# A two-layer DeltaNet backbone on one core: scaling on GpSimd, other store queues, and a TensorE order fixed only from a layer's second latent phase on

## The chip, the cores and the metric

The kernel runs on one core of a Trainium2 chip. The metric is the device time of one execution in microseconds, as a median over runs.

## The reference

Two layers. Each normalises 2048 latent and 256 context tokens (1024 features), projects them once, and feeds a short gated convolution and a bidirectional gated DeltaNet with 4 heads of 128; both results go through one output projection and are added to the tokens. Cut to what matters here:

```python
def hybrid_layer(xl, xc, c, c_ctx, ..., col_major, ctx_out):
    hl = rms_norm(xl, norm_w) * (1.0 + scale_l) + shift_l      # xl (1, 2048, 1024)
    hc = rms_norm(xc, norm_w) * (1.0 + scale_c) + shift_c      # xc (1, 256, 1024)
    pl = split_proj(to_scan_order(hl, col_major) @ w_in)
    pc = split_proj(hc @ w_in)
    dl = deltanet_inputs(pl[4], pl[5], pl[6], pl[8], pl[9], conv_qkv, a_log, dt_bias, seg_l)
    dc = deltanet_inputs(pc[4], pc[5], pc[6], pc[8], pc[9], conv_qkv, a_log, dt_bias, seg_c)
    ol, oc = bidirectional_gdn(dl, dc, ctx_out)     # latent scans start from the context's final state
    yl = from_scan_order(branch_outputs(pl, ol, conv_a, gdn_norm, seg_l), col_major)
    xl = xl + gate_l * (yl @ w_out)
    ...

def deltanet_inputs(q, k, v, ...):
    qkv = jax.nn.silu(segment_conv(jnp.concatenate([q, k, v], axis=-1), conv_qkv, seg))
    q, k, v = jnp.split(qkv, ...)
    q = l2_normalize(q.reshape(b, n, N_HEADS_DN, HEAD_DK)) * (HEAD_DK ** -0.5)
    k = l2_normalize(k.reshape(b, n, N_HEADS_DN, HEAD_DK))
    ...
```

The factor `nk` of the change is the reciprocal norm of `l2_normalize(k)`.

## The kernel before

Feature tiles lie on 128 partitions. The tokens form five chunks: 0 is the context (256 tokens), 1 and 2 are the first half of the latent tokens (512 each), 3 and 4 the second. A layer runs two calls of `phase` (the first with the context and chunks 1 and 2, the second with chunks 3 and 4: the second latent phase) and then `output`. In a phase, a unit is 128 columns of `w_in`: `split` loads them (L313, into `raw`, two buffers), ScalarE rounds them to `whi` (L314), GpSimd and VectorE form the rest `wlo` (L316), and `project` does 24 matmuls for each chunk (`h` by `whi`, `l` by `whi`, `h` by `wlo`, `d<-...` in the rows) into one of three PSUM banks `d`. A consumer then empties the bank; for q, k and v it is a convolution (L339 to L343), a SiLU (L540, L541) and a store to DRAM (`rec_d<-y`, L542). `prep` turns normalised tokens (`xx`) into the operands `h` and `l`: transposes on TensorE (`c<-ident,xx`), L427 on ScalarE (`hf`), and a rounding and a subtraction (L433).

Between the projections' steps run jobs. The job J{l}c has 8 items, J{l}0 to J{l}3 have 16 each; an item is 128 tokens of one head, and there are 144 in the kernel. In `delta` an item loads q, k, v from `rec_d` (L636, L637, ring of four `rec` tiles, two items ahead) and decay rows (L639), transposes them into a PSUM bank `t` (there are two `t` banks), forms key products, and copies the transposes back into `rec`: L668 sums the squares of k, L669 and L670 (a pow on GpSimd) make the norm's factor `nk` from them, L674 copies, L675 copies with the factor `nk`, L677 puts a product in. L678 stores `rec` on ScalarE's queue. Then small triangular systems are solved (`Lt`, `X`; L735, L737), whose tiles of 1024 columns have the tag `m4` (two buffers). The jobs F{l}a to F{l}c and C{l} are scans over the chunks' states. `out_weights` loads `w_out` in two halves of four row tiles into `raw` (L966), rounds them (L967) and forms the rest (L968).

TensorE's order is written by hand over the whole kernel, in one `tc.manual_schedule` over this engine (L1163): it executes in the order in which the code emits, which `phase` and the jobs' `yield`s set by a running count of TensorE's own time (`Order.now`). The order on the other engines and on SP's queue comes from the Tile scheduler, and is fixed once the kernel is built.

Of the kernel before, what the change touches and what calls it, by code (L numbers as in the profile page):

```python
# [8 lines left out]
F32 = mybir.dt.float32  # L9
# [3 lines left out]
ALU = mybir.AluOpType  # L13
# [50 lines left out]
def hybrid_backbone_kernel(ctx_stack: ExitStack, tc: tile.TileContext,  # L64
# [346 lines left out]
    def prep(L, p, i, xx, keep):  # L411

        P = L.P
        r = 1 if p == 0 else 0
        hi, lo = L.hs[p]
        o = slice(128 * i, 128 * i + 256)
        for k2 in range(0, KT, 2):
            with urgent():
                ps = pscan(("c0", "c1")[k2 // 2 % 2]) if p else pt()
                for dk in range(2):  # L420
                    for j in range(2):
                        c_ = 256 * dk + 128 * j
                        turn(ps[:, c_:c_ + 128], xx[:, j, 128 * (k2 + dk):128 * (k2 + dk) + 128])
                hf = side([128, 2, 256], "hf")
                for dk in range(2):
                    k = k2 + dk
                    nc.scalar.activation(hf[:, dk, :], ps[:, 256 * dk:256 * dk + 256], AF.Identity,  # L427
                                         scale=P["am"][:, k, r:r + 1], bias=P["mod"][:, k, r:r + 1])
                if keep:
                    nc.sync.dma_start(out=L.h_d[:, k2:k2 + 2, o], in_=hf)  # L430
                h_ = hi[:, k2:k2 + 2, o]
                nc.vector.tensor_copy(h_, hf)
                (nc.gpsimd if k2 == 6 else nc.vector).tensor_sub(lo[:, k2:k2 + 2, o], hf, h_.bitcast(F32))  # L433
            yield PIECE

    def chunks_in(L, ps, loaded=()):
# [93 lines left out]
    def qkv_unit(L, s, h):  # L530

        par = L.P["par"]
        cw = [par[:, 44 + 12 * j + 4 * s + h:45 + 12 * j + 4 * s + h] for j in range(3)]

        def consume(ci, a):
            g0, n = CHUNKS[ci]
            W = 128 * n
            y = cp.tile([128, 512], F32, tag="y", bufs=YB, name="y")[:, 0:W]
            conv(y, a, cw, NCTX if ci == 0 else L.seg)
            nc.scalar.activation(a, y, AF.Tanh, scale=0.5)  # L540
            nc.vector.scalar_tensor_tensor(y, a, 1.0, y, ALU.add, ALU.mult)  # L541
            nc.sync.dma_start(out=L.rec_d[g0:g0 + n, :, h, REC[s]:REC[s] + 128].rearrange("g p t -> p g t"), in_=y.rearrange("p (g t) -> p g t", t=128))  # L542
        return 2048 + 512 * s + 128 * h, consume

    def zb_unit(L, h):
# [72 lines left out]
    def delta(L, items, with_out, before, wants={}, fast=False):  # L618
# [28 lines left out]
        for i, (h, g) in enumerate(items):  # L647
# [9 lines left out]
            with urgent():  # L657
# [14 lines left out]
                if with_out:  # L672
                    nc.scalar.activation(jk, tp[:, 0:128], AF.Square, accum_out=L.ssq[:, g, h:h + 1])
                nc.scalar.copy(rec[:, 2, :], tp[:, 128:256])  # L674
                nc.scalar.activation(rec[:, 0, :], tp[:, 256:384], AF.Copy, scale=nk[:, i:i + 1])  # L675
                if with_out:
                    nc.vector.tensor_mul(rec[:, 1, :], kp[:, 128:256], dm)  # L677
                nc.scalar.dma_start(out=L.rec_d[g, :, h, 0:384], in_=rec.rearrange("p s t -> p (s t)"))  # L678
            yield ITEM
        held.discard("items")  # L680
        if before is not None:
# [273 lines left out]
    def in_turn(*gens):  # L955
        for name, g in gens:
            yield from g
            done.add(name)

    def out_weights(L, k4, wo):  # L960
        with urgent():
            hi = hp.tile([128, 4, D], F32R, tag="h", bufs=2, name="who")
            lo = hp.tile([128, 4, D], F32R, tag="l", bufs=2, name="wlo")
            for k in range(k4, k4 + 4):
                raw = wp.tile([128, D], F32, tag="raw", bufs=RAWB, name="raw")
                nc.sync.dma_start(out=raw, in_=w_out[L.l][128 * k:128 * k + 128])  # L966
                nc.scalar.copy(hi[:, k - k4, :], raw)  # L967
                nc.vector.tensor_sub(lo[:, k - k4, :], raw, hi[:, k - k4, :].bitcast(F32))  # L968
                wo[k] = (hi[:, k - k4, :], lo[:, k - k4, :])
# [104 lines left out]
    def layer(L, nxt):  # L1074
# [55 lines left out]
        else:  # L1130
# [5 lines left out]
        behind((f"J{l}1", f"C{l}1", ("h", l, 4)), f"F{l}a", lambda: scan(L, 0, lat[:8], 0), "rc")()  # L1136
        behind((f"F{l}a", f"J{l}3"), f"F{l}b", lambda: scan(L, 0, lat[8:], 0), "rc")()
        behind((f"F{l}b",), f"F{l}c", lambda: scan(L, 1, lat[::-1], 1), "rc")()
        wo = {}
        jobs = {("unit", qkv[0]): J(2, *(("mods",) if l == 0 else ())), ("unit", qkv[5]): flag("qkv", l, 1, 1),  # L1140
                ("unit", qkv[8]): J(3), ("unit", qkv[11]): flag("qkv", l, 1, 3),
                ("chunk", 3): lambda: out_weights(L, 0, wo), ("chunk", 4): lambda: out_weights(L, 4, wo)}
        phase(L, units, edge(qkv[:5], 3, 4) + pairs(qkv[5:] + sum(mix, []), (3, 4)) + edge(zb, 3, 4), jobs)
        at_tile = {}
        tiles = list(range(NG - 1, 1, -1))
        if L.ctx_out:
            tiles = [0, 1] + tiles

            def start_next():
                def gen():  # L1150
                    vectors(nxt.l, nxt.P)
                    tables(nxt)
                    yield from mod_job(nxt.l, nxt.P, 0, 12)
                    yield from chunks_in(nxt, (0,))
                spawn("next", gen())
            at_tile[1] = start_next

        def first_weights():
            if nxt is not None:
                nxt.ready = {j: weights(w_in[nxt.l], qkv_unit(nxt, *j)[0], True) for j in ((1, 0), (2, 0))}  # L1160
        output(L, wo, tiles, at_tile, first_weights)

    with tc.manual_schedule(engines={mybir.EngineType.PE}):  # L1163
        constants()
        L = layers[0]
        for l in range(LAYERS):
# [50 lines left out]
```

## Time and profile before

| | |
|---|---|
| median of 3 runs | 2907.5 us (2897.54 to 2908.94) |
| the profiled execution | 2902.76 us, its span 2901.0 us |
| TensorE's mean granted clock in it | 0.964 of full speed |
| busy: TensorE / VectorE / ScalarE / GpSimd | 2642.5 / 1702.8 / 1157.8 / 955.7 us |

All rows are of the profiled execution. The span is the time between its first and last recorded instruction. An engine is busy while an instruction of its own runs; the rest is waiting. Layer 0 fills the span to about 1554 us, where the first three context units of layer 1 are done; the second latent phases begin near 703 and 2087 us.

### The profile page before, as it was taken

What the parts mean: (1) busy time and instruction counts of PE and PEld (TensorE: products, weight loads), DVE (VectorE), ACT (ScalarE), POOL (GpSimd) and SP (SyncE); (2) the same over time, 40 slices, a digit from 0 to 9 for tenths busy, and PEclk for the clock granted to TensorE, in tenths of its full rate; (3) what the DMA queues carried; (4) which work ended last, traced back from release to release, by engine and by line L of the source; (5) the groups of instructions that cost most, each with busy time, mean ns of one, the idle gap of its engine ahead of it and who ended that gap; (6) DMA issues with size and microseconds to landing.
All of it is one profiled execution on the core that took longest, in us unless ns stands there. A gap on an engine that the chain in (4) does not pass through costs nothing. (4 is left out here: it accounts for less than half of the span.)

```text
span 2901.0 us, 48660 instructions
## 1 busy us (share of the span) xinstructions
PE 2642.5 (91%) x17459; PEld 2200.8 (76%) x17459; DVE 1702.8 (59%) x4273; ACT 1157.8 (40%) x3090; POOL 955.7 (33%) x895
## 2 busy tenths in 40 slices
PE   5798889998999899899997888999899999988998
PEld 3676768886877778778786666788787777877787
DVE  3777775325668654455434676774466865446665
ACT  2545452125455322343313444523445542244442
POOL 1322332133223322254444323323222332224543
PEclk9899999999999999999998999999999999999999
DMA  6555843344666536689655446642467652566863
GB/s 212 152 146 160 247 132 90 90 147 144 193 208 190 128 79 225 218 283 328 227 162 174 136 136 185 186 97 71 148 180 221 177 128 65 199 230 236 269 206 110
DMA packets 594158, 501.69 MB, mean 173 GB/s; under 512 B 102410, under 2 KB 549372, under 8 KB 585212
## 3 DMA queue, kind: packets, MB, share of 16 engines
q1 hardware_dynamic: 573180, 470.26, 54.4%
q10 hardware_dynamic: 20736, 28.32, 2.7%
q8 instruction: 138, 2.26, 0.3%
q14 instruction: 104, 0.85, 0.1%
HBM read 368.81 MB, written 129.66 MB: 172 GB/s over the span
## 5 line engine op out<-in xcount | busy, mean ns | idle before, releaser
L155 PE MATMUL d<-h,whi 128*128 128x512 f32 x2048 | 872.8, 426 | 38.7 <-ACT whi L314 31.4
L155 PE MATMUL d<-h,wlo 128*128 128x512 f32 x2048 | 817.1, 399 | 10.4 <-DVE wlo L316 8.9
L155 PE MATMUL d<-l,whi 128*128 128x512 f32 x2048 | 814.0, 397 | 0.0
L316 POOL TENSOR_TENSOR wlo<-raw,whi 128x1024 fp32r<-128x1024 f32 (+1 forms) x176 | 369.9, 2102 | 687.1 <-ACT whi L314 623.9
L155 PEld LDWEIGHTS d<-h,whi 128*128 128x128 f32 x2048 | 395.7, 193 | 120.2 <-ACT whi L314 35.0
L155 PEld LDWEIGHTS d<-h,wlo 128*128 128x128 f32 x2048 | 393.6, 192 | 104.0 <-DVE wlo L316 13.9
L155 PEld LDWEIGHTS d<-l,whi 128*128 128x128 f32 x2048 | 395.7, 193 | 71.5
L155 PE MATMUL d<-who,yy 128*128 128x512 f32 x1088 | 377.3, 406 | 0.0
L314 ACT CAST whi<-raw 128x1024 fp32r<-128x1024 f32 x176 | 184.1, 1046 | 281.1 <-PE d L155 139.6
L155 PEld LDWEIGHTS d<-who,yy 128*128 128x128 f32 x1088 | 206.8, 190 | 44.0 <-issue 4.9
L155 PE MATMUL d<-wlo,yy 128*128 128x512 f32 x544 | 213.9, 393 | 0.0
L670 POOL TENSOR_TENSOR nk<-nk,phalf 128x1 f32<-128x1 f32 x144 | 89.6, 622 | 376.0 <-DVE nk L669 334.9
L841 POOL TENSOR_SCALAR_AFFINE_SELECT rc<-rc 128x512 f32<-128x512 f32 x140 | 91.0, 674 | 257.0 <-DMA rc<-rec_d 211.7
L735 DVE TENSOR_TENSOR tmp<-Lt,X 64x31 f32<-64x31 f32 (+15 forms) x310 | 132.1, 426 | 48.2 <-DMA Lt<-blk 42.4
L737 DVE TENSOR_TENSOR X<-X,tmp 64x31 f32<-64x31 f32 (+15 forms) x310 | 132.4, 427 | 6.6
L540 ACT ACTIVATE d<-y 128x512 f32<-128x512 f32 (+1 forms) x116 | 65.4, 564 | 139.6 <-DVE y L343 123.9
L155 PEld LDWEIGHTS d<-wlo,yy 128*128 128x128 f32 x544 | 103.7, 191 | 16.1
L912 ACT ACTIVATE w<-c,cs 128x128 f32<-128x128 f32 x272 | 78.0, 370 | 91.0 <-DVE wk L908 88.6
L155 PE MATMUL d<-hc,whi 128*128 128x256 f32 x320 | 96.3, 301 | 17.2 <-DVE y L541 15.7
L162 PE MATMUL t<-ident,rec 128*128 128x128 f32 x424 | 74.2, 284 | 40.0 <-ACT rec L675 39.8
L1008 POOL TENSOR_TENSOR yy<-ys,yy 128x512 fp32r<-128x512 f32 x68 | 95.9, 1422 | 40.6 <-ACT yy L1007 39.4
L908 DVE TENSOR_SCALAR wk<-c,cs 128x128 f32<-128x128 f32 x288 | 81.4, 343 | 47.3 <-PE c L155 46.9
(399 smaller groups left out, 4670.6 us busy)
## 6 DMA issues: line engine op xcount, KB each, us to landing
rc<-rec_d SPq DMA_DIRECT2D x68, 1536.0 KB, 7.4
raw<-in_w_in_dram SPq DMA_DIRECT2D x176, 512.0 KB, 4.6
rec_d<-rec ACTq DMA_DIRECT2D x144, 192.0 KB, 3.1
wm<-in_w_mod_dram SPq DMA_DIRECT2D x24, 1024.0 KB, 7.8
rec_d<-y SPq DMA_DIRECT2D x96, 256.0 KB, 2.7
rows<-row_d SPq DMA_DIRECT2D x144, 128.0 KB, 3.8
rec<-rec_d SPq DMA_DIRECT2D x136, 128.0 KB, 2.9
ys<-y_d SPq DMA_DIRECT2D x68, 256.0 KB, 2.9
```

What stands on the lines that cost most here:

```text
L155: nc.tensor.matmul(o, a, b, start=start, stop=stop)
L162: nc.tensor.transpose(o, a, ident[0:a.shape[0], 0:a.shape[0]])
L314: nc.scalar.copy(hi, raw)
L316: eng.tensor_sub(lo[:, k], raw[:, k], hi[:, k].bitcast(F32))
L540: nc.scalar.activation(a, y, AF.Tanh, scale=0.5)
L670: nc.gpsimd.tensor_tensor(nk[:, i:i + 1], nk[:, i:i + 1], phalf[:, 0:1], ALU.pow)
L735: nc.vector.tensor_tensor(t3, L3[:, j + 1:32, j:j + 1].to_broadcast([2 * nb, m_, k]), X3[:, j:j + 1, 0:k].to_broadcast([2 * nb, m_, k]), A ...
L737: nc.vector.tensor_sub(X3[:, j + 1:32, 0:k], X3[:, j + 1:32, 0:k], t3)
L841: nc.gpsimd.affine_select(out=m, in_=m, pattern=[[0, NH], [1 - 2 * d, 128]], compare_op=ALU.is_ge, fill=0.0, base=0, channel_multiplier=2 ...
L908: nc.vector.tensor_scalar(wk[:, h, :], at(p2, h), cs(2 + d, h), None, ALU.mult)
L912: nc.scalar.activation(w[:, h, :], at(p2, h), AF.Copy, scale=cs(d, h))
L1008: nc.gpsimd.tensor_sub(l_, yr, h_.bitcast(F32))
```

## The change

- L675 copies without the factor; a new instruction on GpSimd (L676 after) multiplies `rec` by `nk` in place.
- The store of `rec` moves from ScalarE's queue to SP's (L678 before, L679 after).
- `prep`'s fourth subtraction (L433, 18 in the kernel) moves from GpSimd to VectorE.
- In layer 1's context phase the stores of `y` (L542) move from SP's queue to ScalarE's.
- `out_raws`: at the end of chunk 3 two row tiles of `w_out` (4 and 5) are loaded into `m4` tiles, and the second call of `out_weights` uses them.
- `manual_schedule` now stands around the second latent phase and the output of each layer alone; in front of them the scheduler orders TensorE too.

```diff
-                (nc.gpsimd if k2 == 6 else nc.vector).tensor_sub(lo[:, k2:k2 + 2, o], hf, h_.bitcast(F32))
+                nc.vector.tensor_sub(lo[:, k2:k2 + 2, o], hf, h_.bitcast(F32))
...
-            nc.sync.dma_start(out=L.rec_d[g0:g0 + n, :, h, REC[s]:REC[s] + 128].rearrange("g p t -> p g t"), in_=y.rearrange("p (g t) -> p g t", t=128))
+            (nc.scalar if L.l and ci == 0 else nc.sync).dma_start(out=L.rec_d[g0:g0 + n, :, h, REC[s]:REC[s] + 128].rearrange("g p t -> p g t"), in_=y.rearrange("p (g t) -> p g t", t=128))
...
-                nc.scalar.activation(rec[:, 0, :], tp[:, 256:384], AF.Copy, scale=nk[:, i:i + 1])
+                nc.scalar.copy(rec[:, 0, :], tp[:, 256:384])
+                nc.gpsimd.tensor_scalar(rec[:, 0, :], rec[:, 0, :], nk[:, i:i + 1], None, ALU.mult)
                 if with_out:
                     nc.vector.tensor_mul(rec[:, 1, :], kp[:, 128:256], dm)
-                nc.scalar.dma_start(out=L.rec_d[g, :, h, 0:384], in_=rec.rearrange("p s t -> p (s t)"))
+                nc.sync.dma_start(out=L.rec_d[g, :, h, 0:384], in_=rec.rearrange("p s t -> p (s t)"))
...
+    def out_raws(L, wo):
+
+        with urgent():
+            for k in (4, 5):
+                wo["raw", k] = dp.tile([128, D], F32, tag="m4", bufs=2, name="raw")
+                nc.sync.dma_start(out=wo["raw", k], in_=w_out[L.l][128 * k:128 * k + 128])
...
             for k in range(k4, k4 + 4):
-                raw = wp.tile([128, D], F32, tag="raw", bufs=RAWB, name="raw")
-                nc.sync.dma_start(out=raw, in_=w_out[L.l][128 * k:128 * k + 128])
+                raw = wo.pop(("raw", k), None)
+                if raw is None:
+                    raw = wp.tile([128, D], F32, tag="raw", bufs=RAWB, name="raw")
+                    nc.sync.dma_start(out=raw, in_=w_out[L.l][128 * k:128 * k + 128])
...
+        with tc.manual_schedule(engines={mybir.EngineType.PE}):
+            wo = {}
...
+                    ("chunk", 3): lambda: (out_raws(L, wo), out_weights(L, 0, wo)), ("chunk", 4): lambda: out_weights(L, 4, wo)}
+            phase(L, units, edge(qkv[:5], 3, 4) + pairs(qkv[5:] + sum(mix, []), (3, 4)) + edge(zb, 3, 4), jobs)
...
+            output(L, wo, tiles, at_tile, first_weights)
...
-    with tc.manual_schedule(engines={mybir.EngineType.PE}):
+    if True:
         constants()
```

What the change moves is seen in the order in which each engine executes. The first place is ScalarE in the first latent phase of layer 1, at the fifteenth item of J0 (`t` is the bank with the item's transposes, `d` that of a projection). Before:

```order
L314 CAST whi<-raw 128x1024
L339 ACTIVATE y<-d_81,par 128x512
L668 ACTIVATE rec,ssk<-t_85 128x128
L673 ACTIVATE rec,ssq<-t_85 128x128
L674 COPY rec<-t_85 128x128
L540 ACTIVATE d_81<-y 128x512
L675 ACTIVATE rec<-t_85,nk 128x128
L678 DMA rec_d<-rec 128x384
```

and after the change:

```order
L668 ACTIVATE rec,ssk<-t_85 128x128
L673 ACTIVATE rec,ssq<-t_85 128x128
L314 CAST whi<-raw 128x1024
L674 COPY rec<-t_85 128x128
L675 COPY rec<-t_85 128x128
L339 ACTIVATE y<-d_82,par 128x512
L540 ACTIVATE d_82<-y 128x512
```

The two copies out of the bank now stand side by side, the second does not read `nk`, and the store is gone from this queue.

The second place is TensorE at the start of layer 1, between the third and the fourth context unit (`hc`, `lc` are the context's operands, `xx` the tokens of chunk 1). Before:

```order
L155 MATMUL d_81<-hc,whi 128x256
L155 MATMUL d_81<-lc,whi 128x256
L155 MATMUL d_81<-hc,wlo 128x256
L155 MATMUL d_82<-hc,whi 128x256
L155 MATMUL d_82<-lc,whi 128x256
```

and after the change:

```order
L155 MATMUL d_81<-hc,wlo 128x256
L162 MATMUL c_86<-ident,xx 128x128
L162 MATMUL c_87<-ident,xx 128x128
L162 MATMUL c_86<-ident,xx 128x128 x3
L162 MATMUL c_87<-ident,xx 128x128 x3
L162 MATMUL c_86<-ident,xx 128x128 x4
L162 MATMUL c_87<-ident,xx 128x128 x4
L155 MATMUL d_82<-hc,whi 128x256
```

Sixteen transposes of chunk 1 have moved into this place from behind the context units.

The third place is SP's queue in the second latent phase of layer 0, during J2. Before:

```order
L636 DMA rec<-rec_d 128x128
L637 DMA rec<-rec_d 128x256
L313 DMA raw<-in_w_in_dram 128x8x128
L639 DMA rows<-row_d 128x2x128
L542 DMA rec_d<-y 128x4x128
L639 DMA rows<-row_d 128x2x128
L636 DMA rec<-rec_d 128x128
L637 DMA rec<-rec_d 128x256
```

and after the change:

```order
L679 DMA rec_d<-rec 128x384
L639 DMA rows<-row_d 128x2x128
L636 DMA rec<-rec_d 128x128
L637 DMA rec<-rec_d 128x256
L313 DMA raw<-in_w_in_dram 128x8x128
L639 DMA rows<-row_d 128x2x128
L679 DMA rec_d<-rec 128x384
L542 DMA rec_d<-y 128x4x128
L639 DMA rows<-row_d 128x2x128
L636 DMA rec<-rec_d 128x128
L637 DMA rec<-rec_d 128x256
```

The stores of `rec` now stand in SP's queue, each ahead of the loads into the same buffer; the other rows keep their order.

On GpSimd a scaling (L676) follows each of the 144 pows (L670), directly in 126 places; in 9 a weight split (L316) stands between the two. On TensorE the rows are the same as before from the logits of chunk 3 to the first context units of layer 1, and from the logits of chunk 3 in layer 1 to the end; there the trace of before shows 703 to 1554 us and 2087 to 2901 us.

## Rows read from the trace of the kernel before

**Rows 1.** The page, part 1: busy time and share of the span, instructions

```profile
span 2901.0 us, 48660 instructions
PE 2642.5 (91%) x17459; PEld 2200.8 (76%) x17459; DVE 1702.8 (59%) x4273; ACT 1157.8 (40%) x3090; POOL 955.7 (33%) x895
```

**Rows 2.** TensorE's waits, 100 to 703: waited for, us, times, longest

```profile
PE t L162 <- ACT rec L675: 14.3, 8, 4.6
...
PE t L155 <- ACT rec L675: 4.2, 2, 2.3
```

**Rows 3.** TensorE's waits, 703 to 1554

```profile
PE t L162 <- ACT rec L675: 9.2, 4, 4.5
...
PE t L155 <- ACT rec L675: 2.4, 1, 2.4
```

**Rows 4.** TensorE's waits, 1554 to 2087

```profile
PE d L155 <- DVE y L541: 15.0, 2, 12.9
PE t L162 <- ACT rec L675: 13.7, 6, 4.0
PE c L162 <- ACT hf L427: 11.6, 6, 5.0
...
PE t L155 <- ACT rec L675: 3.6, 2, 3.2
```

**Rows 5.** TensorE's waits, 2087 to 2901

```profile
PE d L155 <- ACT whi L314: 8.4, 1, 8.4
PE t L162 <- ACT rec L675: 6.9, 3, 4.8
PE o L155 <- ACT q__23954 L917: 4.6, 1, 4.6
...
PE t L155 <- ACT rec L675: 4.0, 1, 4.0
```

**Rows 6.** Line L675: what its engine sat idle until (us, times)

```profile
POOL nk L670: 84.3, 86
```

**Rows 7.** Timeline around one stall: start, us, instruction [idle before <-releaser]

```profile
1781.85 0.27 ACT L674 COPY rec<-t 128x128 f32<-128x128 f32 x1
...
1782.75 2.35 POOL L316 TENSOR_TENSOR wlo<-raw,whi 128x1024 fp32r<-128x1024 f32 x1
...
1785.05 0.73 POOL L670 TENSOR_TENSOR nk<-nk,phalf 128x1 f32<-128x1 f32 x1
...
1785.81 0.37 ACT L675 ACTIVATE rec<-t,nk 128x128 f32<-128x128 f32 x1 [2.29 <-POOL nk L670]
...
1786.21 0.33 ACTq L678 DMA_DIRECT2D rec_d<-rec  x1
...
1786.23 0.90 PE L162 MATMUL t<-ident,rec 128*128 128x128 f32 x3 [3.97 <-ACT rec L675]
```

**Rows 8.** Windows of that stall: each engine's busy us, then PEclk, DMA share, GB/s

```profile
1786.00:1788.00 2.00, 1.76 (x6) 1.58 (x7) 0.00 (x0) 0.18 (x1) 0.00 (x0) 0.50 0.55 124
1788.00:1790.00 2.00, 2.00 (x12) 1.71 (x11) 1.45 (x10) 1.37 (x6) 0.91 (x2) 0.67 1.08 343
```

**Rows 9.** Timeline at the start of layer 1, TensorE and ScalarE

```profile
1560.11 1.06 ACT L298 ACTIVATE junk<-xx 128x1024 bf16<-128x1024 f32 x1 [3.20 <-DMA xx<-x]
...
1566.93 0.58 PE L155 MATMUL d<-hc,whi 128*128 128x256 f32 x1 [12.91 <-DVE y L541]
```

**Rows 10.** GpSimd and VectorE instructions by line: duration ns min/median/max

```profile
L701 POOL TENSOR_SCALAR bs<-tri_u,cl x72: 447/471/1297, 181.8 to 2373.0; 128x128 f32<-128x128 f32 x72
```

**Rows 11.** Groups of instructions by line: busy us, mean ns

```profile
L433 POOL TENSOR_TENSOR l<-hf,h 128x512 fp32r<-128x512 f32 x16 | 21.1, 1320 | 52.9 <-DVE h L432 47.2 <-DVE sm L503 5.7
...
L433 DVE TENSOR_TENSOR l<-hf,h 128x512 fp32r<-128x512 f32 x48 | 33.5, 698 | 0.8
```

**Rows 12.** Waits of SP's queue: waited for, us, times, longest

```profile
SPq L636 <- DMA rec_d<-rec: 214.2, 94, 8.4
```

**Rows 13.** DMA issues: count, KB each, median us from issue to landing

```profile
rec_d<-rec ACTq DMA_DIRECT2D x144, 192.0 KB, 3.1
```

More of the change, by code (lines that the diff above doesn't have):

```diff
@@ L1138, in layer @@
         behind((f"F{l}b",), f"F{l}c", lambda: scan(L, 1, lat[::-1], 1), "rc")()
[L1139 to L1160, printed above, removed]
@@ L1161, in layer, with start_next, gen, first_weights @@
-        output(L, wo, tiles, at_tile, first_weights)
-    with tc.manual_schedule(engines={mybir.EngineType.PE}):
+        with tc.manual_schedule(engines={mybir.EngineType.PE}):
+            wo = {}
+            jobs = {("unit", qkv[0]): J(2, *(("mods",) if l == 0 else ())), ("unit", qkv[5]): flag("qkv", l, 1, 1),
+                    ("unit", qkv[8]): J(3), ("unit", qkv[11]): flag("qkv", l, 1, 3),
+                    ("chunk", 3): lambda: (out_raws(L, wo), out_weights(L, 0, wo)), ("chunk", 4): lambda: out_weights(L, 4, wo)}
+            phase(L, units, edge(qkv[:5], 3, 4) + pairs(qkv[5:] + sum(mix, []), (3, 4)) + edge(zb, 3, 4), jobs)
+            at_tile = {}
+            tiles = list(range(NG - 1, 1, -1))
+            if L.ctx_out:
+                tiles = [0, 1] + tiles
+                def start_next():
+                    def gen():
+                        vectors(nxt.l, nxt.P)
+                        tables(nxt)
+                        yield from mod_job(nxt.l, nxt.P, 0, 12)
+                        yield from chunks_in(nxt, (0,))
+                    spawn("next", gen())
+                at_tile[1] = start_next
+            def first_weights():
+                if nxt is not None:
+                    nxt.ready = {j: weights(w_in[nxt.l], qkv_unit(nxt, *j)[0], True) for j in ((1, 0), (2, 0))}
+            output(L, wo, tiles, at_tile, first_weights)
```

## The prediction

> **What bounds the kernel now.** First the page's busy times: TensorE is busy 2642.5 of 2901.0 us, VectorE 59%, ScalarE 40%, GpSimd 33% [rows 1]. So the time is TensorE's work plus about 258 us in which it idles, and the work stays: the change adds no matmul and takes none away. What can change is the idle time, the order of the work, and the clock. Second, the view of what TensorE waited for, in four stretches: the new order is free in 0 to 703 and 1554 to 2087 us and fixed, row for row as now, in 703 to 1554 and 2087 to 2901. Among the waits shown stands one line in every stretch, L675, for which the transposes (L162) and the key products (L155) of a later item wait: 14.3 + 4.2 [rows 2], 9.2 + 2.4 [rows 3], 13.7 + 3.6 [rows 4], 6.9 + 4.0 [rows 5], together 58.3 us in 27 waits, 2.2 us each. Third, the view of line L675 itself: ScalarE stood before it 84.3 us in 86 waits for the pow on GpSimd, L670 [rows 6]. L675 is the last reader of its PSUM bank `t`, there are two such banks, so a late pow holds the bank, and TensorE with it.
>
> Fourth, the timeline of one such stall, at the fifteenth item of J0 of layer 1 [rows 7]. ScalarE ends the other copy (L674) at 1782.12. GpSimd then works 2.35 us on a weight split (L316), does the pow from 1785.05, L675 runs at 1785.81, and TensorE's transposes follow at 1786.23 after 3.97 us of waiting. Fifth, the windows behind the stall: after those 3.97 us of standing the granted clock is 0.50 (the lower level, 1.2 GHz) for 2 us, and 0.67 on average in the 2 us after that: 1.0 + 0.7 = 1.7 us of full-rate work lost on top [rows 8].
>
> **The change, part by part.**
>
> *A, the bank (L675 becomes a plain copy, the scaling moves to GpSimd).* The copy doesn't read the pow's result. In the stall above it could have ended at 1782.12 + 0.27 = 1782.39 (L674's duration) in place of 1786.18, and 3.8 of 3.97 us would be gone. Not every wait on L675 is a wait on the pow: ScalarE's order of work ahead of it stays. Bounds: 0 (the bank is held by something else anyway) and all 58.3. I take three quarters, **-44 us**; the waits on the pow are many more (86) than TensorE's waits on the bank (27), so most of the 27 should be of that kind.
>
> *Clock.* The 27 waits would be 15 or fewer of a length that costs clock (58.3/3.97 = 15 stalls like the one shown). 15 x 1.7 = 25 is the bound, 0 the other. I take five: that many rows have a longest wait of 4.0 to 4.8 us [rows 2 to 5], **-9 us**.
>
> *B, the start of layer 1.* TensorE stands 12.91 us in front of the fourth context unit, because ScalarE waits for the token tiles (3.20 us before L298) ahead of the first consumers [rows 9]. Later in the stretch the transposes of the next chunk wait 11.6 us in six for `hf` [rows 4]. The new order puts 16 of these transposes into the first gap: at 0.90/3 = 0.3 us each [rows 7] that is 4.8 us of work in idle time, and the later waits lose their cause. Both together are 16.4, one bound. The other is +4.8, if the fourth unit is ready and stands behind the transposes. I take half, **-8 us**.
>
> *C, the other order of the free phases.* Where its matmuls, in the order before and after, are added up at their full-rate durations, items stand 5.5 to 6 us of TensorE's work apart where they stood 4 apart. So each producer has more time; the first items move by 14 to 43 us of work to the back, and the end of J1 by 3 to 4 only. From below: the 15.0 us on `d<-y` could go [rows 4], less what B has counted, about -10. From above: the new order meets other late producers; one wait of the present mean, 2.2 us, in every fourth of 80 items is +44. I take **0**, because neither side has a row for it.
>
> *D, the scaling and the store in series.* The nearest row to the new instruction is L701, a GpSimd scaling of the same shape: 447/471/1297 ns [rows 10]. It replaces the 0.37 us of L675 in front of the store, so the store comes 0.1 us later, or 0.93 at worst. 144 x 0.47 = 68 us brings GpSimd from 955.7 to 1023, 35%. The store moves from ScalarE's queue to SP's, where the load for the buffer's next user already waits for that same store's landing, 214.2 us in 94 waits [rows 12]. SP now also waits in front of the store, but the load behind it could not have gone anyway. Landing takes 3.1 us [rows 13]; two items ahead are loaded, some 8 us of cover at 4 us an item. Bounds: 0 and 64 items of the fixed phases x 0.93 = +60. I take a twelfth, **+5 us**, since the median is the smaller one and the cover is longer than the sum of it. If the cover is gone, item by item 0.93 us at most appears on TensorE, and rival 2 is what happens. By the Trainium skill (SBUF — State Buffer, "SBUF: two separate sides") GpSimd and a VectorE operation with two SBUF inputs exclude each other for a whole instruction; the spread of L701 from 0.447 to 1.297 us agrees with it, and with the upper value throughout D would be +60 in place of +5. The stores of `y` in layer 1's context phase go to ScalarE's queue (8 of them, 0.33 us each by the store in [rows 7]): 2.6 us of an engine that is 40% busy, nothing.
>
> *E, two rows of w_out loaded early.* They fill two of the four tiles of the second half. The large wait, 8.4 us for `whi`, comes from the first half and stays; what can shrink is a 4.6 us wait behind it [rows 5]. Two layers: 0 to -9.2. I take **-2 us**.
>
> *F, 18 subtractions from GpSimd to VectorE.* 0.698 against 1.320 us [rows 11]: 0.6 us shorter in the chain of each, 13 us more on VectorE (59% busy). They lie beside projections: **0**, bounds +-5.
>
> *G, what comes back.* A stall that goes lets TensorE run into the next one: splits (`whi`, `wlo`) and bank waits that were long over. I give back two fifths of A and the clock, 0.4 x 53 = **+21 us**; bounds 0 and all of it, +53.
>
> Sum: -44 - 9 - 8 + 0 + 5 - 2 + 0 + 21 = -37 us. The profiled execution took 2902.76 us (1.8 more than its span), 4.7 below the median of the three runs, 2907.5, and inside their spread. 2902.8 - 37 = **2866 us**.
>
> **Rivals.** *1, slower: the frozen order meets late producers.* In the front phases TensorE's order was paced by hand against its own work; now it is what the scheduler's clock thought best, and TensorE executes it in order. Where the real producer (GpSimd's pow, a load behind SP's waits) is later than assumed, each of the 80 items there can stop TensorE. At 2.2 us a wait it decides from 37/2.2 = 17 waits more; with a wait at every second item it is 40 x 2.2 = +88 on 2866, 2954 us. For it: present stretches have waits of 2 to 5 us at several producers. Against: items stand further apart than now, so a producer has more time.
>
> *2, no change: SP stands in front of stores.* If the 0.93 of D or two thirds of it, 0.6 us, reach TensorE at each of the 64 items of the fixed phases, where the order can't give way, that is +38, and 2904 us comes out. For it: SP's order is strict, and 214 us of its waits are of this kind [rows 12]; a split of 2.35 us between pow and scaling [rows 7] delays the store and all loads behind it. Against: only in 9 of 144 items does a split stand between the two.
>
> *3, a larger gain.* All 58.3, 25 of clock, 16 of B, 9 of E, and nothing given back: 2903 - 108 = 2795 us. For it: VectorE and ScalarE have room. Against: waits that vanish entirely in 27 of 27 places aren't likely with the same `whi` and `wlo` behind them.
>
> *4, the change does nothing:* the bank is also held by the transposes' other readers; then A and the clock are 0 and the sum is near 2898, which goes with rival 2.
>
> **How the numbers follow.** Forecast 0.50, with its own range 2835 to 2890 (A between half and all, G between a fifth and three fifths). Rival 3: 0.08. Rivals 2 and 4: 0.20. Rival 1: 0.22. Half a per cent of 2907.5, 14.5 us, is about what a measurement of this kernel can tell from no change: 2893 to 2922 is "same". So faster 0.58, same 0.20, slower 0.22. The range 2805 to 2940 leaves out half of rival 3 and somewhat more than half of rival 1, about 0.17.
>
> **What would show it.** Right: in the trace after, TensorE's waits on L675 in 703 to 1554 and 2087 to 2901, where the order is the same, fall from 22.5 us to under 6; ScalarE no longer stands for the pow before L675; SP's waits in front of the new store are there, but TensorE's waits on loaded `rec` tiles stay under 10 us. The first gap in layer 1 has transposes in it. Granted clock above 0.964. Wrong: waits of TensorE on `rec` loads or on the scaling in the fixed phases (rival 2); more idle time in 0 to 703 or 1554 to 2087 than now, at other producers (rival 1); or the same idle time, under other names, at `whi` and `wlo` (G larger than two fifths).

## The result and the profile after

The changed kernel takes 2863.26 us (median of 3 runs, 2860.83 to 2866.81). The ratio to the kernel before is 0.9859, 95% interval 0.9837 to 0.988. The forecast was 2866 us, the profiled execution's span is 2859.1, 41.9 less than before.

The page of the changed kernel, its first lines:

```profile
span 2859.1 us, 48903 instructions
## 1 busy us (share of the span) xinstructions
PE 2638.3 (92%) x17459; PEld 2196.2 (77%) x17459; DVE 1723.0 (60%) x4291; ACT 1134.4 (40%) x3090; POOL 1033.9 (36%) x1021
```

Against [rows 1] TensorE has the same 17459 instructions and is busy 4 us less, so the gain is idle time: 258 us before, 221 after. Where it went is seen when both executions are cut at the same three places in the program: the logits of chunk 3 in each layer (the first `beta<-t` of that chunk, line L478 on ScalarE) and the first context matmul of layer 1. The first and third stretch are the front phases, which are free now; the second and fourth are the fixed ones. The windows of the kernel before (length, then busy us of TensorE, weight loads, VectorE, ScalarE, GpSimd, then granted clock, DMA share, GB/s):

```profile
0.00:704.88 704.88, 611.41 (x4233) 502.25 (x4234) 401.56 (x1012) 284.13 (x695) 205.35 (x196) 0.96 0.52 152
704.88:1545.21 840.33, 795.11 (x5153) 664.26 (x5152) 467.58 (x1206) 309.19 (x889) 298.15 (x278) 0.98 0.64 200
1545.21:2087.86 542.65, 482.32 (x3308) 395.61 (x3307) 341.39 (x854) 235.02 (x567) 172.42 (x159) 0.94 0.50 141
2087.86:2901.00 813.14, 753.69 (x4772) 638.65 (x4770) 492.32 (x1201) 329.46 (x942) 279.74 (x264) 0.97 0.60 184
```

The same windows of the changed kernel:

```profile
0.00:682.72 682.72, 603.65 (x4228) 497.65 (x4228) 404.99 (x1018) 276.44 (x692) 228.37 (x229) 0.95 0.54 157
682.72:1522.63 839.91, 798.20 (x5156) 667.67 (x5156) 470.05 (x1210) 305.13 (x891) 315.99 (x307) 0.98 0.65 201
1522.63:2044.48 521.85, 479.73 (x3303) 390.72 (x3301) 348.75 (x859) 227.68 (x565) 191.15 (x193) 0.97 0.52 146
2044.48:2859.10 814.62, 756.77 (x4774) 640.20 (x4774) 499.21 (x1204) 325.18 (x944) 298.36 (x294) 0.97 0.60 184
```

By stretch the change is -22.2, -0.4, -20.8 and +1.5 us. All of the gain lies in the two free phases. The two fixed ones gave nothing, although the waits on the bank went there too. TensorE's waits in the second and then in the fourth stretch of the changed kernel:

```profile
PE d L155 <- ACT whi L314: 7.5, 1, 7.5
PE t L162 <- DMA rec<-rec_d: 7.2, 3, 3.2
PE o L155 <- DVE rec L678: 5.5, 2, 4.8
...
PE t L155 <- ACT rec L675: 2.3, 1, 2.3
...
PE d L155 <- ACT whi L314: 8.3, 1, 8.3
PE t L162 <- DMA rec<-rec_d: 5.3, 3, 3.3
...
PE t L155 <- ACT rec L675: 3.9, 1, 3.9
```

The waits on L675 in the fixed phases fell from 22.5 us [rows 3, 5] to 2.3 + 3.9 = 6.2. In their place stand 7.2 + 5.3 = 12.5 us for loads of `rec`, a wait that the views of before don't show in these stretches. SP's queue now waits in front of the new stores, too (waited for, us, times, longest):

```profile
SPq L679 <- POOL rec L676: 72.1, 50, 5.9
```

Over the whole kernel, the view of line L675 after (who waited for it, us, times) has

```profile
  PE t L155: 6.3, 2
...
  PE t L162: 1.6, 4
```

that is 7.9 us in place of 58.3, and no row is left in which ScalarE stands before L675 for the pow, 84.3 us before [rows 6].

So the first theory, that the released bank is the gain, doesn't fit the fixed phases. Its rival is that the free order is the gain, in whatever way the copy is made.

### The profile page after: what moved, and what is told of

It is laid out like the page before. It is cut to its first block, busy times and chain, and to the rows that moved or that the text cites. A ratio compares the mean times of both kernels' runs of the same rounds, so it can differ in the third digit from the quotient of the medians.

```text
span 2859.1 us, 48903 instructions
## 1 busy us (share of the span) xinstructions
PE 2638.3 (92%) x17459; PEld 2196.2 (77%) x17459; DVE 1723.0 (60%) x4291; ACT 1134.4 (40%) x3090; POOL 1033.9 (36%) x1021
## 5 line engine op out<-in xcount | busy, mean ns | idle before, releaser
L155 PE MATMUL d<-h,whi 128*128 128x512 f32 x2048 | 852.2, 416 | 37.9 <-ACT whi L314 20.1
L316 POOL TENSOR_TENSOR wlo<-raw,whi 128x1024 fp32r<-128x1024 f32 (+1 forms) x176 | 369.9, 2102 | 666.3 <-ACT whi L314 635.9
L155 PEld LDWEIGHTS d<-h,whi 128*128 128x128 f32 x2048 | 391.9, 191 | 120.9 <-ACT whi L314 22.2
L670 POOL TENSOR_TENSOR nk<-nk,phalf 128x1 f32<-128x1 f32 x144 | 92.3, 641 | 293.2 <-DVE nk L669 220.9
L736 DVE TENSOR_TENSOR tmp<-Lt,X 64x31 f32<-64x31 f32 (+15 forms) x310 | 142.1, 458 | 43.2 <-DMA Lt<-blk 37.1
L738 DVE TENSOR_TENSOR X<-X,tmp 64x31 f32<-64x31 f32 (+15 forms) x310 | 126.4, 408 | 6.6
L155 PEld LDWEIGHTS d<-wlo,yy 128*128 128x128 f32 x544 | 103.6, 190 | 16.1
L666 ACT ACTIVATE dm<-dm 128x128 f32<-128x128 f32 x144 | 44.6, 311 | 171.2 <-DVE dm L665 167.1
L676 POOL TENSOR_SCALAR rec<-rec,nk 128x128 f32<-128x128 f32 x144 | 101.8, 707 | 26.5 <-issue 8.0
L928 DVE SCALAR_TENSOR_TENSOR S<-S,atot,c 128x128 f32<-128x128 f32 x272 | 76.4, 342 | 55.7 <-PE c L155 55.7
```

Of the source, the lines that this page charges most:

```text
L155: nc.tensor.matmul(o, a, b, start=start, stop=stop)
L316: eng.tensor_sub(lo[:, k], raw[:, k], hi[:, k].bitcast(F32))
L670: nc.gpsimd.tensor_tensor(nk[:, i:i + 1], nk[:, i:i + 1], phalf[:, 0:1], ALU.pow)
L676: nc.gpsimd.tensor_scalar(rec[:, 0, :], rec[:, 0, :], nk[:, i:i + 1], None, ALU.mult)
L736: nc.vector.tensor_tensor(t3, L3[:, j + 1:32, j:j + 1].to_broadcast([2 * nb, m_, k]), X3[:, j:j + 1, 0:k].to_broadcast([2 * nb, m_, k]), A ...
L738: nc.vector.tensor_sub(X3[:, j + 1:32, 0:k], X3[:, j + 1:32, 0:k], t3)
```

## The experiments

Each is compared with runs of the kernel before on the same chip, whose median there was 2899.9 to 2907.9 us, so the ratios are compared, not the medians. The table has the stretches as cut above, from each profiled execution, and the ratio to before with its 95% interval; behind the two front phases stands in brackets TensorE's idle time in them. A stretch is that of one execution, which lies within 6 us of the kernel's median, but for free_only, whose profiled execution took 12.8 us more. The fixed stretches, with the same order, spread over 12 us each between the kernels; the front phases with the order by hand lie between 703.6 and 706.5 and between 539.3 and 549.0 us, apart from the one that strewn_by_hand changes. "Short bunches" is counted in TensorE's order: how often 8 or fewer of the 1440 matmuls of 32x32 stand together between other work.

| kernel | front, layer 0 (idle) | fixed | front, layer 1 (idle) | fixed | median us | ratio | short bunches |
|---|---|---|---|---|---|---|---|
| before | 704.9 (93.5) | 840.3 | 542.7 (60.3) | 813.1 | 2907.5 | 1 | 0 |
| changed | 682.7 (79.1) | 839.9 | 521.9 (42.1) | 814.6 | 2863.3 | 0.9859 (0.9837 to 0.988) | 11 |
| all_by_hand | 706.5 (91.6) | 840.9 | 539.3 (56.9) | 818.6 | 2905.1 | 1.0013 (1.0003 to 1.0023) | 0 |
| free_only | 761.8 (92.7) | 842.8 | 525.0 (44.0) | 811.0 | 2929.7 | 1.0108 (1.0083 to 1.0132) | 91 |
| act_scale | 737.8 (86.4) | 835.5 | 530.6 (45.9) | 809.2 | 2920.1 | 1.007 (1.0048 to 1.0092) | 75 |
| scale_and_free | 702.7 (93.4) | 835.2 | 533.8 (48.2) | 812.2 | 2885.9 | 0.995 (0.9934 to 0.9967) | 4 |
| strewn_by_hand | 726.7 (97.9) | 837.2 | 549.0 (63.4) | 815.5 | 2929.1 | 1.0081 (1.0048 to 1.0113) | 32 |
| free_l1 | 703.6 (95.3) | 841.5 | 531.5 (47.8) | 808.2 | 2890.0 | 0.9949 (0.993 to 0.9969) | 1 |
| no_out_raws | 682.2 (77.4) | 835.3 | 522.1 (38.5) | 815.1 | 2859.4 | 0.9843 (0.9815 to 0.9872) | 9 |
| no_l433 | 702.4 (93.0) | 843.3 | 528.0 (41.6) | 814.8 | 2885.3 | 0.9928 (0.9906 to 0.995) | 9 |
| l433_k4 | 681.6 (77.8) | 844.3 | 524.4 (40.2) | 817.7 | 2868.4 | 0.9865 (0.9833 to 0.9896) | 12 |
| l433_k0 | 691.9 (84.9) | 844.0 | 521.5 (39.8) | 819.7 | 2875.7 | 0.9893 (0.9864 to 0.9923) | 8 |
| act_store | 696.9 (90.3) | 831.8 | 525.9 (40.4) | 807.2 | 2865.7 | 0.9862 (0.9837 to 0.9887) | 10 |
| best_ctx | 681.4 (75.5) | 842.1 | 530.1 (41.4) | 814.8 | 2867.7 | 0.9866 (0.9839 to 0.9893) | 9 |

In layer 1's front phase TensorE idles 56.9 to 63.4 us in every kernel whose order there is by hand, and 38.5 to 48.2 us in every kernel whose order there is free, whichever engine scales. In layer 0's front phase a free order gives between 681.4 and 761.8 us, on either side of the 704.9 by hand; the runs below ask why.

### all_by_hand

```diff
-        with tc.manual_schedule(engines={mybir.EngineType.PE}):
+        if True:
             wo = {}
...
-    if True:
+    with tc.manual_schedule(engines={mybir.EngineType.PE}):
         constants()
```

> The changed kernel with TensorE's order by hand over the whole kernel, as before; the copy, the scaling on GpSimd, the queues and the early rows of w_out stay. In the changed kernel the two phases whose order is fixed gained nothing (840.3 to 839.9 and 813.1 to 814.6 us) and the two free ones 22 and 21 us. Theory of the prediction (the released bank is the gain, wherever it stands): in the front phases the waits on the copy go here too, 25 to 40 us faster than before, about 2870. Rival (the free order is the gain): no change, 2900 to 2912, with waits on the copy replaced by waits on rec loads in all phases.

2905.06 us: no gain. Every part of the change but the order is in it, and together they are worth nothing in the order by hand. TensorE's waits in its two fixed phases:

```profile
PE t L162 <- DMA rec<-rec_d: 6.4, 3, 3.3
...
PE t L162 <- DMA rec<-rec_d: 6.9, 5, 3.1
```

The waits on the copy have become waits on loaded `rec` tiles, as in the changed kernel. The first theory falls, for a kernel that stores on SP's queue. The released bank with the order by hand and the store on ScalarE's queue was not run; act_store, below, has that in its fixed phases alone.

### free_only

The kernel before, with the last part of the change alone (what stands in the region is indented, and as before):

```diff
+        with tc.manual_schedule(engines={mybir.EngineType.PE}):
             wo = {}
...
-    with tc.manual_schedule(engines={mybir.EngineType.PE}):
+    if True:
         constants()
```

> The kernel before with one thing changed: TensorE's order is fixed only from a layer's second latent phase on. Theory of the prediction: the scheduler cannot remove the waits on L675, since the bank is held until the pow; 0 to 10 us faster, 2897 to 2907. Rival (the free order is the gain): 30 to 45 us faster, 2862 to 2877. Third (both are needed): the order alone gives 10 to 20 us.

2929.72 us: slower by 1%, against every one of the expectations. In the profiled execution layer 1's front phase gained 17.7 us, but layer 0's lost 56.9. The loss isn't a wait: TensorE idled there 92.7 us against 93.5 before, and was busy 669.1 against 611.4. Windows from that phase:

```profile
520.00:530.00 10.00, 8.81 (x41) 7.17 (x41) 5.76 (x13) 0.80 (x2) 4.49 (x4) 1.00 0.38 97
530.00:540.00 10.00, 5.31 (x56) 4.33 (x55) 1.43 (x2) 5.51 (x9) 1.04 (x2) 0.71 0.55 115
540.00:550.00 10.00, 10.00 (x31) 5.04 (x31) 0.00 (x0) 0.00 (x0) 0.00 (x0) 0.50 0.00 0
...
600.00:620.00 20.00, 20.00 (x80) 11.15 (x79) 0.69 (x1) 0.00 (x0) 0.00 (x0) 0.50 0.00 0
```

By its records TensorE is busy in every microsecond of the last two windows, and its granted clock is 0.50, the lower level of 1.2 GHz. The timeline says what it did (the first two rows stand ahead of the strewn ones):

```profile
540.32 0.63 PE L155 MATMUL d<-l,whi 128*128 128x512 f32 x1
540.75 0.63 PE L155 MATMUL d<-h,wlo 128*128 128x512 f32 x1
...
548.20 0.80 PE L155 MATMUL d<-h,wlo 128*128 128x512 f32 x1
548.93 0.31 PE L155 MATMUL t<-tf,U 32*32 32x32 f32 x2
549.17 0.80 PE L155 MATMUL d<-h,whi 128*128 128x512 f32 x1
549.90 0.31 PE L155 MATMUL t<-tb,U 32*32 32x32 f32 x2
```

The scheduler has strewn the small matmuls of J1's triangular blocks (steps z1 and va of `delta`), which stand in bunches of 64 and 96 in the order by hand, mostly one by one between single matmuls of the projections (the trace has two records for each of these 32x32 matmuls in f32: 576 for the 288 on `tf`). A round of one projection matmul and one small one takes 549.17 - 548.20 = 0.97 us. At the same half clock a projection's matmul without a small one behind it is followed after 540.75 - 540.32 = 0.43. In the kernel before, in the same phase and at a granted clock of 1.00, it is followed after 0.23:

```profile
536.42 0.39 PE L155 MATMUL d<-h,wlo 128*128 128x512 f32 x1
536.65 0.40 PE L155 MATMUL d<-h,whi 128*128 128x512 f32 x1
```

In 600 to 620 us the small matmuls stand between the context's matmuls of 128x256. The clock did not fall in the same way each time. Between 530 and 540 us, ahead of the strewn matmuls, TensorE was busy 5.31 of 10 us; there it fell, and it stayed low while they ran. The second fall came within a strewn stretch, with no gap in the records (TensorE's busy time, granted clock, DMA share, GB/s):

```profile
575.00:580.00 5.00, 5.00 (x26) 1.00 1.00 301
580.00:585.00 5.00, 5.00 (x22) 0.70 0.06 13
```

### act_scale

```diff
-                nc.scalar.copy(rec[:, 0, :], tp[:, 256:384])
-                nc.gpsimd.tensor_scalar(rec[:, 0, :], rec[:, 0, :], nk[:, i:i + 1], None, ALU.mult)
+                nc.scalar.activation(rec[:, 0, :], tp[:, 256:384], AF.Copy, scale=nk[:, i:i + 1])
...
-                nc.sync.dma_start(out=L.rec_d[g, :, h, 0:384], in_=rec.rearrange("p s t -> p (s t)"))
+                nc.scalar.dma_start(out=L.rec_d[g, :, h, 0:384], in_=rec.rearrange("p s t -> p (s t)"))
```

> The changed kernel with the scaling back in L675 on ScalarE and the store back on ScalarE's queue; the free order, L433, the stores of y and the early rows of w_out stay. Theory of the prediction: the waits on the pow return, 25 to 40 us slower than the changed kernel, 2888 to 2903. Rival (the order is the gain): at most 8 us slower, 2863 to 2871.

2920.14 us, 1.007 of before: slower than either theory said. Its order has 75 short bunches, and again it is layer 0's front phase that is long (737.8). Against the changed kernel that phase is 55.0 us longer, of which 47.7 are busy time and 7.3 idle time. ScalarE stands in front of L675 for the pow again (81.4 us over the kernel), but TensorE's waits on L675 do not come back in the front phases (0.2 and 2.6 us, against 18.5 and 17.3 before), and most of the loss is not a wait: the scaling's place matters here by the order that the scheduler finds with it.

### scale_and_free

The changed kernel without the three small parts, that is the kernel before with the copy, the scaling, the store on SP and the free order (its diff is that of no_out_raws, no_l433 and best_ctx, below, together).

> The kernel before with the copy, the scaling on GpSimd, the store on SP and the free front order, but L433 on GpSimd, the stores of y on SP and no early rows of w_out, as before. Both theories: within 6 us of the changed kernel, 2860 to 2869, since the three small parts were put at 0, 0 and -2. If they carry more, 2870 and above.

2885.87 us: faster than before, but not by the whole amount. The three small parts, which the prediction put at -2 us together, go with 23 us by the medians, 26 by the ratios.

### strewn_by_hand

This asks whether the strewing by itself costs the time. The kernel before, order by hand:

```diff
                 mm(acc, w[i][:, k, :], h[j][:, k, :], start=(k + z == 0), stop=(k + z == KT + 1))
+                if Order.strew and z < 2:
+                    pump()
...
-                for d, a, b in pairs:
+                for t, (d, a, b) in enumerate(pairs):
                     mm(z13[Q(b), i, :], U[i // 8][Q(a), i % 8, 32 * b:32 * b + 32], T[d][Q(a), i, :])
+                    if before == "J00" and t % 2:
+                        Order.strew = True
+                        yield 0.0
+            Order.strew = False
```

> The kernel before, TensorE's order by hand, with one thing changed: in layer 0's job J1 the 64 matmuls of 32x32 of the step z1, which stand in one bunch, are put two by two between single matmuls of the projections (32 bunches of two). The matmuls and what they compute stay. In the free order without the scaling, the scheduler had strewn 91 such short bunches, TensorE's granted clock was 0.50 there while it was busy all the time, and layer 0's front phase took 57 us more. Theory now (strewing small matmuls among the projections costs the clock): the granted clock falls to 0.50 over this stretch, one round of a pair and a projection's matmul takes about 0.97 us in place of 0.25, 20 to 30 us slower than before. Rival (the free order's loss has another source, as waits): within 8 us of before.

2929.1 us, 23.6 above before, as that theory said. In the profiled executions it is 27.4 us, 21.8 of them in layer 0's front phase. Windows around the stretch:

```profile
535.00:540.00 5.00, 5.00 (x45) 1.00 0.01 3
540.00:545.00 5.00, 5.00 (x41) 0.61 0.14 52
545.00:550.00 5.00, 5.00 (x33) 0.50 0.00 0
550.00:555.00 5.00, 5.00 (x32) 0.50 0.00 0
...
560.00:565.00 5.00, 1.69 (x182) 1.00 0.41 120
```

and its timeline while the clock still was at 1.00:

```profile
533.52 0.49 PE L156 MATMUL d<-h,wlo 128*128 128x512 f32 x1
533.95 0.25 PE L156 MATMUL t<-tb,U 32*32 32x32 f32 x4
534.13 0.51 PE L156 MATMUL d<-h,whi 128*128 128x512 f32 x1
```

The cost has two parts. At the full clock a round of one projection matmul and two small ones (four records) takes 534.13 - 533.52 = 0.61 us, where the projection's matmul alone takes 0.23. After some rounds of this, with matmuls of 128x512 and then of 128x256, the clock falls to 0.50, without any gap in the records of TensorE, and it is back at 1.00 after the strewing has ended. The expected 0.97 us for a round did not come: all rounds at half clock have a matmul of 128x256 here, and take 0.76. The Trainium skill (TensorEngine Tiling (Array Packing), "Key Properties") says that changing the tiling mode drains TensorE; the 0.61 us agree with that. That strewing costs clock as well is what the windows show; the one thing that was changed is the strewing.

### free_l1

The kernel before, with the order free in layer 1's front phase alone:

```diff
-        until("next")
-        layer(layers[1], None)
+    until("next")
+    layer(layers[1], None)
```

(and `manual_schedule` in `layer` as in the change).

> The kernel before, scaling on ScalarE, with TensorE's order free in layer 1's front phase alone; the small matmuls stay in bunches there but for one. Theory now (the free order gains by itself where it doesn't strew small matmuls): 12 to 20 us faster than before, about 2880 to 2888, all of it between the first context matmul and the logits of chunk 3 in layer 1. Rival (the released bank is needed for the gain): within 6 us of before.

2890.03 us, ratio 0.9949. In the profiled executions 11.1 of 16.1 us lie in the expected stretch, 542.7 to 531.5; the rest is within the spread of the fixed stretches. So the free order gains without the released bank, where it leaves the small matmuls together. It even takes most of the waits on the bank away, though the copy still waits for the pow (26.6 us in 22 waits in this stretch). Of TensorE's 17.3 us on L675 [rows 4] there are left, between 1545 and 2077 us:

```profile
PE t L162 <- ACT rec L675: 2.1, 2, 1.1
...
PE t L155 <- ACT rec L675: 0.9, 1, 0.9
```

Over all kernels with a free order this stretch takes 525.0 to 531.5 us with the scaling on ScalarE and 521.5 to 533.8 with it on GpSimd, so these runs don't show what the scaling adds here.

### no_out_raws, no_l433

The early rows go in the first; the fourth subtraction of `prep` is back on GpSimd in the second:

```diff
-                    ("chunk", 3): lambda: (out_raws(L, wo), out_weights(L, 0, wo)), ("chunk", 4): lambda: out_weights(L, 4, wo)}
+                    ("chunk", 3): lambda: out_weights(L, 0, wo), ("chunk", 4): lambda: out_weights(L, 4, wo)}
```

```diff
-                nc.vector.tensor_sub(lo[:, k2:k2 + 2, o], hf, h_.bitcast(F32))
+                (nc.gpsimd if k2 == 6 else nc.vector).tensor_sub(lo[:, k2:k2 + 2, o], hf, h_.bitcast(F32))
```

> The changed kernel without the two early rows of w_out. By the prediction: 2 us slower, 2861 to 2869. If the three small parts carried the 23 us by which the kernel without them was slower than the changed one, and this is the part: 2880 to 2886; if each carries a third, about 2871.

> The changed kernel with the fourth subtraction of prep back on GpSimd. By the prediction (term 0): 2858 to 2868. If this is the small part that carries the 23 us: 2880 to 2886.

2859.43 us without the early rows: within its interval the same as the changed kernel. 2885.32 us with the subtraction back: this is the part that goes with most of the loss, 22 us by the medians, 20 by the ratios. In the profiled executions it is 29.3 us, 19.7 of them in layer 0's front phase. There 13.9 us are idle time, and the largest single part of it is a wait for the loads of `wm` (weights of the modulation job), in no_l433 and then in the changed kernel:

```profile
PE d L229 <- DMA wm<-in_w_mod_dram: 23.1, 6, 10.3
...
PE d L229 <- DMA wm<-in_w_mod_dram: 15.9, 5, 9.1
```

### l433_k4, l433_k0

Is it the time of 18 subtractions on GpSimd, or the order that the scheduler finds with them? The same load, another quarter:

```diff
-                nc.vector.tensor_sub(lo[:, k2:k2 + 2, o], hf, h_.bitcast(F32))
+                (nc.gpsimd if k2 == 4 else nc.vector).tensor_sub(lo[:, k2:k2 + 2, o], hf, h_.bitcast(F32))
```

(`k2 == 0` in the other).

> The changed kernel with another one of prep's four subtractions, the third, on GpSimd; GpSimd's and VectorE's load is that of the run with the fourth one there, which took 2885. Theory now (a small part acts by the order that the scheduler then finds, not by its own time): anywhere between 2855 and 2900, and not the same as 2885 within 4 us. Rival (18 subtractions on GpSimd cost the time themselves): 2881 to 2889.

> The changed kernel with the first of prep's four subtractions on GpSimd, the load again that of the run with the fourth one there. Theory now: not bound to 2885, its difference lies in the two free phases, and the fixed ones stay within 5 us of the changed kernel's. Rival (the subtraction's own time): 2881 to 2889.

2868.38 and 2875.71 us. With the same GpSimd load the time is 2868, 2876 or 2885, and layer 0's front phase 681.6, 691.9 or 702.4, so the load isn't the cause. In l433_k0 the two fixed phases are 4.1 and 5.1 us longer than the changed kernel's, the second just over the 5 that were expected. By hand, with the subtraction on VectorE, nothing was gained (all_by_hand).

What is left is the order, and the traces bear it out for layer 0's front phase. Compared row by row, TensorE's order there is the same in the changed kernel, no_out_raws and best_ctx, but for one place and for records that are missing, and the three take 682.7, 682.2 and 681.4 us. It is the same, in this sense, in no_l433 and scale_and_free, and the two take 702.4 and 702.7. Between the two groups about a quarter of the rows stands in other places. An order as good can look quite different, though: that of l433_k4 shares about three quarters of its rows with the changed kernel's and takes 681.6.

### act_store

```diff
-                nc.sync.dma_start(out=L.rec_d[g, :, h, 0:384], in_=rec.rearrange("p s t -> p (s t)"))
+                nc.scalar.dma_start(out=L.rec_d[g, :, h, 0:384], in_=rec.rearrange("p s t -> p (s t)"))
```

> The changed kernel with the store of rec back on ScalarE's queue, the scaling still on GpSimd. In the fixed phases TensorE waited 12.5 us for rec loads where it waited 22.5 on the copy before. If SP, standing in front of stores, makes these loads late: the waits on rec loads in the fixed phases fall under 5 us, and these two phases get 5 to 10 us shorter together. Rival (the loads are late because the ring of four gives its buffers back late, whoever stores): the fixed phases stay within 3 us. The free phases may move either way by their order.

2865.74 us: the same in sum as the changed kernel, by two movements that cancel. The windows of its fixed phases:

```profile
696.94:1528.70 831.76, 795.58 (x5156) 665.48 (x5156) 470.37 (x1210) 305.84 (x891) 316.77 (x307) 0.98 0.65 203
...
2054.63:2861.80 807.17, 755.20 (x4774) 638.06 (x4774) 496.33 (x1204) 326.69 (x944) 298.69 (x294) 0.97 0.61 186
```

Together 1638.9 us, 15.6 less than the changed kernel's 1654.5 (more than the 5 to 10 that were expected) and 14.5 less than before's 1653.5. Over the other kernels that scale on GpSimd and store on SP the sum of the two lies between 1647.3 and 1663.6, over those that scale and store on ScalarE between 1644.7 and 1653.9. This one lies below all of them, by 8.4 to 24.7 and by 5.8 to 15.0 us; more than that one execution of each can't say. No wait on loaded `rec` tiles is left among TensorE's waits there, so it was SP's queue, and not the ring of four, that made these loads late. What it gained, its front phases lost (+14.2 and +4.1), with another order.

### best_ctx

no_out_raws with the context stores of layer 1 back on SP as well:

```diff
-            (nc.scalar if L.l and ci == 0 else nc.sync).dma_start(out=L.rec_d[g0:g0 + n, :, h, REC[s]:REC[s] + 128].rearrange("g p t -> p g t"), in_=y.rearrange("p (g t) -> p g t", t=128))
+            nc.sync.dma_start(out=L.rec_d[g0:g0 + n, :, h, REC[s]:REC[s] + 128].rearrange("g p t -> p g t"), in_=y.rearrange("p (g t) -> p g t", t=128))
```

> The changed kernel without the early rows of w_out and with the context stores of layer 1 back on SP, that is the copy, the scaling, the store on SP, the fourth subtraction on VectorE and the free order alone. Theory now: the two parts left out carry nothing of their own, 2852 to 2868. Rival (the early rows or the context stores carry part of the gain): 2870 or more.

2867.67 us, at the upper end of what was expected: within the intervals the same as the changed kernel. Against no_out_raws, which differs by the context stores alone, it is 8 us more, and in the profiled executions 8.0 us lie in layer 1's front phase, whose order is another one; the intervals of the two ratios overlap. So the early rows carry nothing, and the context stores nothing that these runs can tell from an order.

## Why the prediction was right, point by point

The time, the sign and the range were right, but that the sum came within 3 us is luck. The forecast gain was A with the clock and G, -32 us net, and B, with C at nothing. Of the 58.3 us of waits that A was to remove 22.5 lie in the fixed phases, so by its own working some 12 us of the gain should have shown there (an estimate, 22.5/58.3 of 32). There the time changed by +1.1. What A was to give, D took back, and the gain of 43.0 us came in the two free phases, where the prediction's own term for the order was 0.

*A, the bank, and G, what comes back.* The waits went as forecast, from 58.3 to 7.9 us, more than the three quarters; but free_l1 and act_scale show that in the front phases the free order takes away most of them without the released bank. The net worth shows in act_store's fixed phases, where the order is the same and the store is not on SP: 14.5 us less than before, 5.8 to 15.0 less than the kernels that scale and store on ScalarE, for 22.5 us of waits. The 12 us of the estimate lie within that; G's two fifths agree with it, but one execution can't test them.

*D, the store on SP.* This term was mis-sized: +5 us, with bounds 0 and +60. It is about 15.6 in the fixed phases (act_store against the changed kernel, one execution each; 8.4 to 24.7 against all kernels that store on SP), and it took back the whole of what A had gained there. It is rival 2's mechanism, at a smaller price than its 38: the waits on loaded `rec` tiles, 12.5 us, passed the mark of 10 that was to show it. In at least six of the 64 items the cover of two items ahead was not longer than the chain from store to load. The scaling itself, priced at 0.47 us by [rows 10], took 0.61; the line's view after, ns min/median/max:

```profile
L676 POOL TENSOR_SCALAR rec<-rec,nk x144: 600/611/3237, 132.6 to 2318.1; 128x128 f32<-128x128 f32 x144
```

*C, the free order.* This step failed. It was put at 0, with bounds -10 and +44, as if order by itself had one price. It has several: 11.1 us gained in layer 1 alone (free_l1), 56.9 lost in layer 0 with the scaling on ScalarE (free_only), 22.2 gained there in the changed kernel and 2.2 in scale_and_free. Rival 1 had the sign of free_only right and its cause wrong: no late producer, but small matmuls strewn among large ones.

*B, the start of layer 1.* -8 us. From the first context matmul to the first latent projection it was 1598.8 - 1545.2 = 53.6 us and is 1570.0 - 1522.6 = 47.4: -6.2, near enough. The transposes do stand in the gap and wait there now, and the sixteen take 4.6 us, close to the 4.8 of the forecast. TensorE's timeline in the changed kernel:

```profile
1537.53 0.69 PE L162 MATMUL c<-ident,xx 128*128 128x128 f32 x2 [6.11 <-DVE xx L408]
1541.62 1.54 PE L162 MATMUL c<-ident,xx 128*128 128x128 f32 x6 [3.40 <-DVE ss L299]
1544.67 2.33 PE L162 MATMUL c<-ident,xx 128*128 128x128 f32 x8 [1.51 <-ACT hf L427]
...
1570.03 0.50 PE L155 MATMUL d<-h,whi 128*128 128x512 f32 x1 [1.07 <-DVE y L541]
```

The 12.91 us of [rows 9] are now 6.11, 3.40 and 1.51 with work between them.

*Clock.* -9 us; TensorE's busy time fell by 4.2 (2642.5 to 2638.3), and the mean granted clock went from 0.964 to 0.966. The changed kernel's three runs lie between 0.963 and 0.969 and those of before between 0.961 and 0.968, so no gain of clock is shown.

*E, the early rows.* -2 us; nothing can be told from zero (no_out_raws). *F, the subtractions.* 0 for their own time, which the runs with equal load don't contradict; but the order that goes with them is worth up to 22 us, and no term had that.

*The prediction's own signs* were split. ScalarE no longer stands for the pow, and the first gap has transposes in it. The waits on L675 in the fixed phases stopped at 6.2 us, just over its mark of 6, and those on `rec` loads went over theirs.

What stays open: why the scheduler strews the blocks when ScalarE scales and leaves them together when GpSimd does, and which of the differences in the order of layer 0's front phase make 682 or 702 us. Open is also what the released bank is worth in the front phases with the order by hand and the store on ScalarE's queue. A kernel that stores on SP in the front phases and on ScalarE in the fixed ones was not run; from the stretches of the changed kernel and of act_store its estimate is 682.7 + 831.8 + 521.9 + 807.2 = 2843.6 us of span, if the front phases keep their order.

## What to carry to other kernels

Cut two traces at the same places of the program before any wait is explained: here one table of stretches showed that the waits named by the prediction had gone where nothing was gained. When a scheduler's order is set free, look first at what it does to bunches of small matmuls, and give an order by itself no price without a run, since a change of equal load moved the time by 17 us. A store that is put on the queue of the loads behind it can be paid for by the loads, as here, so price the chain from store to next load, and not the store's issue.

## What the runs showed that was not expected

A TensorE that the profile shows busy all the time can be granted half its clock: 0.50 over 540 to 560 and 600 to 620 us of free_only, while matmuls of 128x512, and in the second stretch of 128x256, alternated with single ones of 32x32. A round with 128x512 took 0.97 us at half the clock, against 0.43 for the large matmul alone, and with two small ones 0.61 us at the full clock, against 0.23.

A free order can also take waits away that were put down to a late producer: in free_l1 the waits on L675 in layer 1's front phase fell from 17.3 to 3.0 us while the copy still waited for the pow. The same GpSimd work, placed on another quarter of the same loop, gave 2868, 2876 or 2885 us.
